# Attention in two interleaved halves, rotating product banks and a deeper weight queue in a one-core encoder step

## The chip, the cores and the metric

The kernel runs on one core of a Trainium2 chip. The core has five engines with instruction streams of their own: TensorE (in the profile PE, with its weight loads as PEld), VectorE (DVE), ScalarE (ACT), GpSimd (POOL) and SyncE (SP), which here only issues DMAs. The metric is device time in microseconds of one execution; for the kernel before, it is the median of three runs. A profile records one further execution with every instruction's start and duration.

## What is computed

One inference step of a small hybrid encoder: 512 new frames of one stream (the prompt) and 8 running streams with 16 frames each (the sample), 640 rows of width 2048 in all. A first layer (mixer A) projects 2048 to 2 x 4096, applies causal pooling over windows of 2, 4, 8 and 16 frames, a linear map per group, a gate, and projects back. Then keys, values and a forget logit per head are computed once (16 heads of 128), and a second layer (mixer B) does attention over them:

```python
def fox_attention(q, k, v, Fq, Fk, q_pos, k_pos):      # F = cumsum(log f) of the forget gates
    s = jnp.einsum('bqhd,bkhd->bhqk', qb, k) * HEAD_DIM ** -0.5
    s = s + Fq[..., None] - Fk_t[:, :, None, :]
    s = jnp.where(k_pos <= q_pos, s, -jnp.inf)
    p = jax.nn.softmax(s, axis=-1)
    o = jnp.einsum('bhqk,bkhd->bqhd', p, v)

z = rmsnorm(x) @ w_in_b                                 # queries | gate
x = x + (fox_attention(...) * silu(gate)) @ w_out_b
y = rmsnorm(x)
```

The sample rows also attend to 256 cached frames of their stream. All arrays are float32. The kernel gets float32 accuracy from three products of a faster format: each operand is split into a high and a low part (`split`, line 80: ScalarE copies the high part, VectorE subtracts), and high x high, high x low and low x high are added up.

## The kernel before

The 640 rows lie along the free dimension in two halves of 320 (`HALF`), so a product has 128 x 128 weights and 320 moving columns. TensorE's instructions run in the order in which the program writes them (`tc.manual_schedule`, line 174); the order on VectorE, ScalarE, POOL and SP is set by the framework's scheduler, ahead of time. All accumulators are slices of one tensor `banks` of eight banks (line 49).

**Input pairs and K/V pairs.** Both use a Strassen-like scheme with seven products per pair of output blocks. `pair8` (line 258) issues them for four weight slabs of 512 KB; the seven accumulators are banks 0 to 6 in the order `ORDER`, and `tbank()` gives bank 7 to transposes and other small products. `combine` (line 277) then adds and subtracts the seven banks: ScalarE copies m1, VectorE does the rest. Small pieces of other work are generators in the list `work`; `tick()` (line 88) runs the next one up to its `yield`. In `pair8` there are two ticks a slab, after products 2 and 5 (line 271), eight a pair. Thirty-one pairs belong to mixer A's input, sixteen (`kv_pair`, line 1018) to K/V.

**The forget logits** are products of the last residual stream with 16 columns of `w_kv`. `forget_sums(c)` (line 782) adds the two row blocks of stream pair c into banks 6 and 7, a strip of 32 partitions for each k mod 4, while the last output products of mixer A run. Pair 7 comes after the start of K/V: the hook of the first K/V pair calls `last_rows` (line 862), which does `forget_sums(7)`, copies the two banks to `lt`, and splits the last stream blocks. `norm_stream` (line 871) and `forget` (line 883) follow as ticks; `lt` is used in line 925.

**Attention.** Per head there is a query block and a gate block, each a projection of 2048 rows (`proj`, line 1116): four chunks of weights, 16 row blocks, six products each (`mm3`, line 1066, profile line L1069). `chunk()` (line 1111) hands over one split chunk, starts the split of one that comes later and the load of one later still. A split is a scaling of the raw weights by the norm's gain (L1090, VectorE), a copy (L1098, ScalarE) and a subtraction (L1100, VectorE); `prime()` (line 1103) leaves two split chunks in hand, in three buffers. The generator `attn(h, q_)` (line 1226) holds all of a head's attention and is run by nine ticks a projection:

- `turn_keys` transposes cached keys on VectorE (L1232); `running` (L1237) multiplies them with the sample's queries into bank 4;
- `new(t)` (line 1240) makes the scores of prompt block t in bank 4 or 5 and their softmax (L1251 to L1259), in tile `pr[t]`;
- `turn_new(t)` (line 1261) transposes `pr[t]` on TensorE into `tbank()`, here a ring of banks 6 and 7, and splits it (L1269, L1270);
- the sample's probabilities are transposed, then come its values (L1347, L1351, bank 4) and the prompt's (L1360 to L1363, bank 5);
- the result goes to `og` (L1364, L1367) and is multiplied by the gate on VectorE (L1371).

Head h's generator runs beside its own gate block and the next head's query block; the new queries may only be written when `new(3)` of head h is out (`qdone`). Loads of the next head's keys, values and sums are issued from within the generator, on SP.

**Output projection** (line 1456 on): 960 products of 512 columns; its first weights come through the same `chunk()`.

Of the kernel before, what the change touches and what calls it, by code (L numbers as in the profile page):

```python
# [17 lines left out]
P = 128  # L18
# [21 lines left out]
def tile_yoco_step(ctx, tc, i, o):  # L40
# [213 lines left out]

    def tbank():
# [484 lines left out]
    for n, (kind, g, p) in enumerate(units):  # L740
        if n == 1:
            work.append(load_cols())
        if n == 31:
# [38 lines left out]
    def forget_sums(c):  # L782
        for k in (2 * c, 2 * c + 1):
            q = k % 4
            for n in range(2):
                nc.tensor.matmul(banks[32 * q : 32 * q + 32, 6 + n, :HALF], wr[0][:, k * H : k * H + 32],
                                 stage[c][:, k % 2, n * HALF : (n + 1) * HALF], start=k < 4, stop=k >= 12)
# [21 lines left out]
    for g in range(4):  # L809
# [23 lines left out]
        dk = nd  # L833
    for j in range(4, 7):
# [17 lines left out]
    lt = pv.tile([P, NT], F32, name="lt")  # L852
    Fs = pv.tile([P, 5, H], F32, name="Fs")
# [7 lines left out]

    def last_rows():

        forget_sums(7)
        nc.scalar.activation(lt[:, :HALF], banks[:, 6, :HALF], AF.Copy)
        nc.vector.tensor_copy(lt[:, HALF:], banks[:, 7, :HALF])
# [167 lines left out]

    ones = make_ones(pv, "ones")
# [11 lines left out]
    mmring, tring = Ring([0, 2]), Ring([6, 7])  # L1047
    R = big.tile([P, NT], F32, name="R")
    dma(R, Rd)
# [9 lines left out]
    def wchunk(src, nk, nn, scale=None, pin=False):  # L1059
        raw = wp.tile([P, nk, nn], F32, tag="raw", name="raw", bufs=4)  # L1060
        dma(raw, src)
        hi, lo = (wp.tile([P, nk, nn], F32R, tag=q, name=q, bufs=3) for q in ("whi", "wlo"))
# [53 lines left out]
    def proj(ticks=9):  # L1116
# [8 lines left out]
        return pp  # L1125

# [4 lines left out]
    queue(winb, 0, nb_c)  # L1131
    for h in range(H):
        queue(winb, D + h * P, nb_c)
        if h < H - 1:
            queue(winb, (h + 1) * P, nb_c)
    for k in range(H):
        bloads.append((woutb[:, k, :512].unsqueeze(1), None))

    with ExitStack() as ctx2:
# [17 lines left out]
        def load_new_values(h):  # L1157
            vn = pb.tile([P, TT, P], F32, tag="vn", name="vn")
            dma(vn, sv[h].rearrange("(t p) d -> p t d", p=P))
            store(o["v_prompt"][0, :, h, :].rearrange("(t p) d -> p t d", p=P), vn[:, :4, :])  # L1160
# [4 lines left out]
            vals[h] = [vn, vh, vl]  # L1165
# [30 lines left out]
        def gate_block(h):  # L1196
            pp = proj(9 if h < H - 1 else 16)
# [26 lines left out]
        cached, gates, qdone = {}, [], []  # L1224

        def attn(h, q_):
            more = h < H - 1
            kc = cached[h][0]

# [31 lines left out]
            def turn_new(t):  # L1261
                kw = (t + 1) * P
                ts = slice(t * P, kw)
                a = tbank()
                for j in range(t + 1):
                    transpose(a[:, j * P : (j + 1) * P], pr[t][:, j * P : (j + 1) * P])
                n = min(t + 1, 3)
                av = a[:, : n * P].rearrange("p (j q) -> p j q", q=P)
                nc.scalar.activation(pth[:, :n, ts], av, AF.Copy)  # L1269
                nc.vector.tensor_tensor(ptl[:, :n, ts], av, pth[:, :n, ts].bitcast(F32), op=ALU.subtract)  # L1270
                if t == 3:
                    nc.scalar.activation(pt3, a[:, 3 * P :], AF.Copy)

            kct = pk.tile([P, NB * P], F32, tag="kct", name="kct")
# [3 lines left out]
            if h:  # L1278
                yield
            turn_keys(kct, 0, 1)  # L1280
            yield
            while not q_:
                yield
            qt, qh, ql, qs = q_
            kt, kh, kl = keys[h]
            fk = sums[h]
            s2 = pk2.tile([P, 2 * PAST + NS], F32, tag="s2", name="s2")
            pr = [pk2.tile([P, (t + 1) * P], F32, tag=f"p{t}", name="pr") for t in range(4)]
# [10 lines left out]
            yield  # L1299
            new(1)  # L1300
            yield
            running(ss, kct, 1)
# [13 lines left out]
            yield  # L1316
            new(2)
            pth = pk2.tile([P, 3, NP], F32R, tag="pth", name="pth")
            ptl = pk2.tile([P, 3, NP], F32R, tag="ptl", name="ptl")
            turn_new(0)  # L1320
            yield
            new(3)
            qdone.append(h)
            if more:
                split_new_keys(h + 1)
                load_sums(h + 1)
            yield
            turn_new(1)
            pt3 = pk2.tile([P, P], F32, tag="p0", name="pt3")
            yield  # L1330
            pts = pk2.tile([P, 5, P], F32, tag="pts", name="pts")
            turn_new(2)
            yield
            for js in ((0, 1, 2, 3), (4,)):
# [3 lines left out]
                nc.scalar.activation(pts[:, js[0] : js[-1] + 1].rearrange("p j n -> p (j n)"), a[:, : len(js) * P], AF.Copy)  # L1338
                yield
            turn_new(3)  # L1340
            yield
            vc = cached[h][1]
            vn, vh, vl = vals[h]
            po = banks[:, 4, :]
# [7 lines left out]
            ob = pk2.tile([P, P], F32, tag="ob", name="ob")  # L1352
            nc.vector.tensor_copy(ob, po[:, :P])
# [3 lines left out]
            op = banks[:, 5, :]  # L1357
# [5 lines left out]
            nc.tensor.matmul(op[:, 3 * P :], vn[:, 3, :], pt3, start=False, stop=True)  # L1363
            nc.scalar.activation(og[:, h, :NP], op, AF.Copy)  # L1364
            a = tbank()
            transpose(a[:, :P], ob)
            nc.scalar.activation(og[:, h, NP:], a[:, :P], AF.Copy)  # L1367
            if more:
                load_new_values(h + 1)
            sg = gates.pop()  # L1370
            nc.vector.tensor_tensor(og[:, h, :], og[:, h, :], sg, op=ALU.mult)  # L1371
# [4 lines left out]
        prime()  # L1376
        load_keys(0)
        load_new_keys(0)
        split_new_keys(0)
# [3 lines left out]
        q_ = []  # L1383
        work.append(attn(0, q_))
        for h in range(H):
            q_.extend(q_block(h))
            if h:
                work.append(attn(h, q_))
            gate_block(h)
            q_ = []  # L1390
        while work:
            tick()
# [128 lines left out]
```

## Time and profile before

| | |
|---|---|
| median of 3 runs | 2921.6 us (2912.43 to 2922.14) |
| profiled execution: time, span of its instructions | 2911.26 us, 2909.3 us |
| TensorE busy | 2780.2 us (96%) |
| VectorE busy | 2014.5 us (69%) |
| ScalarE busy | 1149.5 us (40%) |
| POOL busy | 382.2 us (13%) |
| mean granted TensorE clock | 0.985 |

Rows of groups read: line, engine, operation, output <- inputs, shapes, count | busy us, mean ns of one | idle time of the engine just before them and what ended it. Rows of time begin with start and duration in us. "Idle" of TensorE is time in which no matmul was under way; a busy TensorE can still run at a reduced clock, which the stage table shows. A line number can be that of a helper (L81 and L84 are the two halves of `split`, L105 is `transpose`).

### The profile page before, as it was taken

What the parts mean: (1) busy time and instruction counts of PE and PEld (TensorE: products, weight loads), DVE (VectorE), ACT (ScalarE), POOL (GpSimd) and SP (SyncE); (2) the same over time, 40 slices, a digit from 0 to 9 for tenths busy, and PEclk for the clock granted to TensorE, in tenths of its full rate; (3) what the DMA queues carried; (4) which work ended last, traced back from release to release, by engine and by line L of the source; (5) the groups of instructions that cost most, each with busy time, mean ns of one, the idle gap of its engine ahead of it and who ended that gap; (6) DMA issues with size and microseconds to landing.
All of it is one profiled execution on the core that took longest, in us unless ns stands there. A gap on an engine that the chain in (4) does not pass through costs nothing. (4 is left out here: it accounts for less than half of the span.)

```text
span 2909.3 us, 46312 instructions
## 1 busy us (share of the span) xinstructions
PE 2780.2 (96%) x18194; PEld 2651.2 (91%) x18194; DVE 2014.5 (69%) x3430; ACT 1149.5 (40%) x1911; POOL 382.2 (13%) x357
## 2 busy tenths in 40 slices
PE   7899999999999999999998999998999999999998
PEld 6799999999999999999998999987888888888787
DVE  7877778887786858584567888875665665656434
ACT  5433333333233435353345555542433433435222
POOL 2112131322420111112023111110000000000000
PEclk8999999999999999999999999999999999999999
DMA  3344444444345877779443554556555554545923
GB/s 124 114 130 134 132 124 129 128 131 125 112 130 164 200 166 182 171 180 182 139 145 89 117 127 117 121 123 152 138 129 128 134 131 118 133 126 110 144 85 110
DMA packets 646755, 390.69 MB, mean 134 GB/s; under 512 B 322756, under 2 KB 601716, under 8 KB 646408
## 3 DMA queue, kind: packets, MB, share of 16 engines
q1 hardware_dynamic: 626952, 333.99, 43.4%
q0 software_dynamic: 19584, 53.75, 8.6%
q8 instruction: 142, 2.33, 0.3%
q14 instruction: 77, 0.63, 0.1%
HBM read 299.66 MB, written 87.99 MB: 133 GB/s over the span
## 5 line engine op out<-in xcount | busy, mean ns | idle before, releaser
L251 PE MATMUL banks<-b,wh 128*128 128x320 f32 x2688 | 602.7, 311 | 16.7 <-ACT cve L289 10.6
L251 PE MATMUL banks<-th,wh 128*128 128x320 f32 x1792 | 566.9, 316 | 9.5 <-DVE cu L293 4.6
L251 PE MATMUL banks<-th,wl 128*128 128x320 f32 x1792 | 557.3, 311 | 2.8 <-DVE wl L84 2.8
L251 PE MATMUL banks<-tl,wh 128*128 128x320 f32 x1792 | 557.6, 311 | 0.7 <-DVE tl L84 0.7
L251 PEld LDWEIGHTS banks<-b,wh 128*128 128x128 f32 x2688 | 452.5, 189 | 18.3 <-ACT cve L289 11.6
L251 PE MATMUL banks<-b,wl 128*128 128x320 f32 x1344 | 417.2, 310 | 0.0
L84 DVE TENSOR_TENSOR wl<-raw,wh 128x768 fp32r<-128x768 f32 (+1 forms) x264 | 308.5, 1170 | 143.0 <-ACT wh L81 139.7
L81 ACT ACTIVATE wh<-sums 128x1024 fp32r<-128x1024 f32 x224 | 236.3, 1055 | 371.0 <-DVE sums L220 370.8
L81 ACT ACTIVATE wh<-raw 128x768 fp32r<-128x768 f32 (+1 forms) x264 | 230.2, 873 | 345.3 <-issue 154.8
L251 PEld LDWEIGHTS banks<-th,wh 128*128 128x128 f32 x1792 | 340.2, 190 | 19.8 <-DVE cu L293 9.1
L1069 PE MATMUL banks<-b,whi 128*128 128x320 f32 x1536 | 358.0, 317 | 0.0
L251 PEld LDWEIGHTS banks<-th,wl 128*128 128x128 f32 x1792 | 339.9, 190 | 3.3 <-DVE wl L84 3.3
L251 PEld LDWEIGHTS banks<-tl,wh 128*128 128x128 f32 x1792 | 340.2, 190 | 1.2 <-DVE tl L84 0.9
L84 DVE TENSOR_TENSOR wl<-sums,wh 128x1024 fp32r<-128x1024 f32 x224 | 282.1, 1259 | 70.6 <-ACT wh L81 70.0
L1069 PEld LDWEIGHTS banks<-b,whi 128*128 128x128 f32 x1536 | 257.8, 191 | 1.2 <-issue 0.4
L251 PEld LDWEIGHTS banks<-b,wl 128*128 128x128 f32 x1344 | 254.1, 189 | 0.0
L1069 PE MATMUL banks<-b,wlo 128*128 128x320 f32 x768 | 197.7, 312 | 0.0
L217 DVE TENSOR_TENSOR sums<-raw 128x512 f32<-128x512 f32 x236 | 174.9, 741 | 11.5 <-POOL sq L769 4.5
L1098 ACT ACTIVATE whi<-raw 128x512 fp32r<-128x512 f32 x144 | 88.9, 628 | 160.7 <-DVE raw L1090 89.8
L1100 DVE TENSOR_TENSOR wlo<-raw,whi 128x512 fp32r<-128x512 f32 x144 | 98.1, 687 | 72.6 <-ACT whi L1098 72.3
L213 ACT ACTIVATE raw<-raw,cols 128x256 f32<-128x256 f32 x256 | 111.1, 497 | 62.1 <-DMA raw<-in_w_kv 62.1
L1069 PEld LDWEIGHTS banks<-b,wlo 128*128 128x128 f32 x768 | 135.4, 190 | 0.0
(395 smaller groups left out, 4864.7 us busy)
## 6 DMA issues: line engine op xcount, KB each, us to landing
raw<-in_w_in_a SPq DMA_DIRECT2D x128, 512.0 KB, 4.0
raw<-in_w_out_a SPq DMA_DIRECT2D x64, 512.0 KB, 5.0
raw<-in_w_kv SPq DMA_DIRECT2D x64, 512.0 KB, 4.1
raw<-in_w_in_b SPq DMA_DIRECT2D x128, 256.0 KB, 3.9
raw<-in_w_grp_a SPq DMA_DIRECT2D x32, 512.0 KB, 5.6
kc<-in_cache_k SPq DMA_DIRECT2D x64, 256.0 KB, 5.3
vc<-in_cache_v SPq DMA_DIRECT2D x16, 1024.0 KB, 5.6
raw<-in_w_out_b SPq DMA_DIRECT2D x64, 256.0 KB, 3.3
```

What stands on the lines that cost most here:

```text
L81: a = nc.scalar.activation(hi, x, AF.Copy)
L84: nc.vector.tensor_tensor(lo, x, hi.bitcast(F32), op=ALU.subtract)
L213: nc.scalar.activation(raw[:, k, :], raw[:, k, :], AF.Copy, scale=loads[n][2][:, k : k + 1])
L217: nc.vector.tensor_tensor(sums[:, :, 0:2, :], raw[:, :, 1:3, :], raw[:, :, 0:1, :].to_broadcast([P, 2, 2, P]), op=ALU.subtract)
L251: nc.tensor.matmul(bank[:, :HALF], w[kk][:, a, :], x, start=first and q == 0, stop=last and q == 2)
L1069: nc.tensor.matmul(acc_[:, s, :HALF], w, stream(k, q, s), start=f, stop=l)
L1098: nc.scalar.activation(hi, raw, AF.Copy)
L1100: nc.vector.tensor_tensor(lo, raw, hi.bitcast(F32), op=ALU.subtract)
```

## The change

**Banks in rotation.** A counter `base` shifts the seven accumulators by seven banks (mod 8) after every pair, and `tbank()` is the eighth bank of the current pair. Ticks move to after products 3 and 6, and the last one of a pair is dropped, seven a pair. `base` is set to 4 before the second pair and to 2 before K/V.

**Forget sums in two parts.** Pairs 0 to 6 are copied from banks 6 and 7 to a tile `forgot` before K/V begins, stored to DRAM and loaded into `lt`. The last pair's products go to `tbank()` in the first K/V pair's hook, one half after product 3 and one after product 6, and VectorE adds them to `lt`.

**Weights.** `whi` and `wlo` get four buffers instead of three, and `prime()` leaves three split chunks. `prime()` now runs right after the weight pool exists, ahead of the loads of `R` and of `Fs`. The query block two heads ahead is queued, and the first two query blocks run before the first gate block.

**Attention in two generators.** `scoring(h)` holds the cached and new scores with their softmax, `valuing(h)` the transposes, the values and the gate product. They stand in the lists `front` and `back`; `step()` serves them in alternation, ten times a projection (sixteen in the last gate blocks). Beside gate block h-1 and query block h+1 run `scoring(h)` and `valuing(h-1)`. The set `turned[h]` tells which probability tiles have been transposed and may be rewritten. The value results use the ring of banks 6 and 7 instead of banks 4 and 5, `pt3` has a tile of its own, the split of the new values moves from their load to the middle of `valuing`, and the gate product moves from VectorE to POOL.

```diff
     def tbank():
-        return banks[:, 7, :]
+        return banks[:, (base[0] + 7) % 8, :]
...
-        pp = {m: banks[:, j, :] for j, m in enumerate(ORDER)}
+        pp = {m: banks[:, (base[0] + j) % 8, :] for j, m in enumerate(ORDER)}
...
-                if j in (2, 5):
+                if j in (3, 6) and n + j < 9:
                     tick()
+        base[0] += 7
...
+    forgot = wa.tile([P, NT], F32, tag="sums", name="forgot")
+    for n in range(2):
+        nc.scalar.activation(forgot[:, n * HALF : (n + 1) * HALF], banks[:, 6 + n, :HALF], AF.Copy)
+    lgd = dram.tile([P, NT], F32, name="lgd")
+    dma(lgd, forgot)
...
     lt = pv.tile([P, NT], F32, name="lt")
+    dma(lt, lgd)
...
+    def last_forget(n):
+        hs = slice(n * HALF, (n + 1) * HALF)
+        tb = tbank()
+        for k in (14, 15):
+            q = k % 4
+            nc.tensor.matmul(tb[32 * q : 32 * q + 32, :HALF], wr[0][:, k * H : k * H + 32], stage[7][:, k % 2, hs],
+                             start=True, stop=True)
+        nc.vector.tensor_tensor(lt[64:, hs], lt[64:, hs], tb[64:, :HALF], op=ALU.add)
...
-        forget_sums(7)
-        nc.scalar.activation(lt[:, :HALF], banks[:, 6, :HALF], AF.Copy)
-        nc.vector.tensor_copy(lt[:, HALF:], banks[:, 7, :HALF])
...
-            if (n, s, j) == (0, 0, 2):
-                last_rows()
+            if (n, s) == (0, 0) and j in (3, 6):
+                last_forget(j // 6)
+                if j == 6:
+                    last_rows()
...
-            hi, lo = (wp.tile([P, 512], F32R, tag=q, name=q, bufs=3) for q in ("whi", "wlo"))
+            hi, lo = (wp.tile([P, 512], F32R, tag=q, name=q, bufs=4) for q in ("whi", "wlo"))
...
-        split_next()
-        fetchb()
-        split_next()
-        fetchb()
+        for _ in range(3):
+            split_next()
+            fetchb()
...
+    def step():
+        turns[0] += 1
+        for q in (front, back) if turns[0] % 2 else (back, front):
+            while q:
+                try:
+                    next(q[0])
+                    return
+                except StopIteration:
+                    q.pop(0)
...
+    prime()
+    R = big.tile([P, NT], F32, name="R")
+    dma(R, Rd)
...
         def q_block(h):
             pp = proj()
-            while h and not qdone:
-                tick()
-            qdone.clear()
+            drain(front)
...
+        def valuing(h):
...
+            for t in range(4):
+                turn_new(t)
+                turned[h].add(t)
+                yield
...
-            po = banks[:, 4, :]
+            po = tbank()
...
-            op = banks[:, 5, :]
+            op = tbank()
...
-            nc.vector.tensor_tensor(og[:, h, :], og[:, h, :], sg, op=ALU.mult)
+            while not gates:
+                yield
+            nc.gpsimd.tensor_tensor(og[:, h, :], og[:, h, :], gates.pop(), op=ALU.mult)
...
-        work.append(attn(0, q_))
-        for h in range(H):
-            q_.extend(q_block(h))
-            if h:
-                work.append(attn(h, q_))
-            gate_block(h)
-            q_ = []
-        while work:
-            tick()
+        q_ = {}
+        q_[0] = q_block(0)
+        front.append(scoring(0, q_[0]))
+        q_[1] = q_block(1)
+        for h in range(1, H):
+            front.append(scoring(h, q_[h]))
+            back.append(valuing(h - 1))
+            gate_block(h - 1)
+            if h < H - 1:
+                q_[h + 1] = q_block(h + 1)
+            drain(front)
+            drain(back)
+        back.append(valuing(H - 1))
+        gate_block(H - 1)
+        drain(back)
```

More of the change, by code (lines that the diff above doesn't have):

```diff
@@ L742, in tile_yoco_step @@
             work.append(load_cols())
+            base[0] = 4
         if n == 31:
@@ L1061, in wchunk @@
         dma(raw, src)
-        hi, lo = (wp.tile([P, nk, nn], F32R, tag=q, name=q, bufs=3) for q in ("whi", "wlo"))
+        hi, lo = (wp.tile([P, nk, nn], F32R, tag=q, name=q, bufs=4) for q in ("whi", "wlo"))
         split(hi, lo, raw, pin)
@@ L1123, in proj, with drain @@
                 if kk * ticks % KT < ticks:
-                    tick()
+                    step()
         return pp
+    front, back, turns = [], [], [0]
+    def step():
[7 more added lines that the diff above has]
+                    q.pop(0)
+    def drain(q):
+        while q:
+            try:
+                next(q[0])
+            except StopIteration:
+                q.pop(0)
     def queue(src, c0, scale):
@@ L1222, in load_values, with scoring @@
             cached[h].append(vc)
-        cached, gates, qdone = {}, [], []
-        def attn(h, q_):
+        cached, gates = {}, []
+        scores = {}
+        def scoring(h, q_):
             more = h < H - 1
             kc = cached[h][0]
+            kct = pk.tile([P, NB * P], F32, tag="kct", name="kct")
             def turn_keys(kct, g, b):
@@ L1259, in new @@
                 nc.vector.tensor_scalar_mul(s, s, rw)
[L1261 to L1274, printed above, removed]
             turn_keys(kct, 0, 0)
@@ L1277, in attn @@
                 load_new_keys(h + 1)
-            if h:
-                yield
+            yield
             turn_keys(kct, 0, 1)
             yield
-            while not q_:
-                yield
             qt, qh, ql, qs = q_
+            if h == 0:
+                split_new_keys(0)
             kt, kh, kl = keys[h]
             fk = sums[h]
-            s2 = pk2.tile([P, 2 * PAST + NS], F32, tag="s2", name="s2")
-            pr = [pk2.tile([P, (t + 1) * P], F32, tag=f"p{t}", name="pr") for t in range(4)]
+            while h and 0 not in turned[h - 1]:
+                yield
+            pr = [pk2.tile([P, P], F32, tag="p0", name="pr")]
             ss = banks[:, 4, :]
@@ L1299, in attn @@
             yield
+            while h and 1 not in turned[h - 1]:
+                yield
+            pr.append(pk2.tile([P, 2 * P], F32, tag="p1", name="pr"))
             new(1)
             yield
+            while h and 5 not in turned[h - 1]:
+                yield
+            s2 = pk2.tile([P, 2 * PAST + NS], F32, tag="s2", name="s2")
             running(ss, kct, 1)
@@ L1316, in attn @@
             yield
+            pr.append(pk2.tile([P, 3 * P], F32, tag="p2", name="pr"))
             new(2)
-            pth = pk2.tile([P, 3, NP], F32R, tag="pth", name="pth")
-            ptl = pk2.tile([P, 3, NP], F32R, tag="ptl", name="ptl")
-            turn_new(0)
             yield
+            pr.append(pk2.tile([P, 4 * P], F32, tag="p3", name="pr"))
             new(3)
-            qdone.append(h)
             if more:
@@ L1326, in attn, with turn_new @@
                 load_sums(h + 1)
+            scores[h] = pr, s2
+            turned[h] = set()
             yield
-            turn_new(1)
-            pt3 = pk2.tile([P, P], F32, tag="p0", name="pt3")
-            yield
-            pts = pk2.tile([P, 5, P], F32, tag="pts", name="pts")
-            turn_new(2)
-            yield
-            for js in ((0, 1, 2, 3), (4,)):
+        turned = {}
+        def valuing(h):
+            more = h < H - 1
+            pr, s2 = scores[h]
+            pth = pk2.tile([P, 3, NP], F32R, tag="pth", name="pth")
+            ptl = pk2.tile([P, 3, NP], F32R, tag="ptl", name="ptl")
+            pt3 = pk2.tile([P, P], F32, tag="pt3", name="pt3")
+            pts = pk2.tile([P, 5, P], F32, tag="pts", name="pts")
+            def turn_new(t):
+                kw = (t + 1) * P
+                ts = slice(t * P, kw)
+                a = tbank()
+                for j in range(t + 1):
+                    transpose(a[:, j * P : (j + 1) * P], pr[t][:, j * P : (j + 1) * P])
+                n = min(t + 1, 3)
+                av = a[:, : n * P].rearrange("p (j q) -> p j q", q=P)
+                nc.scalar.activation(pth[:, :n, ts], av, AF.Copy)
+                nc.vector.tensor_tensor(ptl[:, :n, ts], av, pth[:, :n, ts].bitcast(F32), op=ALU.subtract)
+                if t == 3:
+                    nc.scalar.activation(pt3, a[:, 3 * P :], AF.Copy)
+            for t in range(4):
+                turn_new(t)
+                turned[h].add(t)
+                yield
+            for n, js in enumerate(((0, 1, 2, 3), (4,))):
                 a = tbank()
@@ L1356, in attn @@
             yield
-            op = banks[:, 5, :]
+            ob = pk2.tile([P, P], F32, tag="ob", name="ob")
+            nc.vector.tensor_copy(ob, po[:, :P])
+            op = tbank()
             for j in range(3):
@@ L1366, in attn @@
             transpose(a[:, :P], ob)
+            yield
             nc.scalar.activation(og[:, h, NP:], a[:, :P], AF.Copy)
[L1368 to L1371, printed above, removed]
+            while not gates:
+                yield
+            nc.gpsimd.tensor_tensor(og[:, h, :], og[:, h, :], gates.pop(), op=ALU.mult)
             yield
```

37 lines of the change are left out of this document (19 added, 18 removed).

## The prediction

> **What bounds the kernel now.** I read the page first, then a table of stages, then who makes TensorE wait, and last the stretches around those waits in order of time. Columns of the table: length of the stretch, busy us and instructions of each engine, granted TensorE clock, DMA share, GB/s.
>
> ```profile
> span 2909.3 us, 46312 instructions
> 83.00:886.00 803.00, 785.52 (x5267) 780.44 (x5268) 640.06 (x1019) 286.33 (x405) 201.37 (x205) 0.98 0.43 129
> 958.00:1534.00 576.00, 574.68 (x3908) 567.39 (x3906) 374.43 (x570) 230.35 (x336) 96.57 (x88) 1.00 0.69 167
> 1534.00:1957.00 423.00, 411.06 (x2733) 402.01 (x2733) 348.75 (x508) 223.28 (x389) 63.86 (x43) 0.99 0.49 117
> 1957.00:2680.00 723.00, 660.63 (x4519) 600.75 (x4520) 441.44 (x959) 273.29 (x543) 2.47 (x2) 0.98 0.53 129
> 2680.00:2910.00 230.00, 219.20 (x955) 178.45 (x953) 93.11 (x173) 59.77 (x115) 0.00 (x0) 0.98 0.54 117
> ```
>
> The stretches are mixer A's input pairs, its grouped and output products, the K/V pairs, attention (1957 to 2680) and the output projection. TensorE sets the pace in all of them; what can be won is its idle time: 723.00 - 660.63 = 62.4 us in attention, 17.5 in the input pairs, 11.9 in K/V. VectorE is busy 441.44 of 723.00 (61%) in attention, so it is late at moments and not short of time.
>
> ```profile
> PE banks L1069 <- ACT whi L1098: 36.0, 23, 5.7
> PE banks L105 <- DVE pr L1259: 22.0, 16, 2.0
> PE banks L251 <- ACT cve L289: 10.6, 4, 3.0
> PE banks L251 <- DVE cu L293: 4.6, 2, 2.4
> PE banks L1237 <- DVE kct L1232: 4.5, 2, 2.7
> PE banks L251 <- ACT ub L553: 3.8, 1, 3.8
> PE banks L251 <- DVE cu L290: 3.3, 7, 1.8
> PE banks L877 <- DVE lt L866: 2.8, 1, 2.8
> PE banks L251 <- DVE x L802: 2.3, 1, 2.3
> PE banks L105 <- DVE ptl L1270: 0.9, 1, 0.9
> ```
>
> Columns: total us, times, longest. Attention's idle time is 36.0 (projection products wait for split weights), 22.0 (the transposes of a head's probabilities wait for its softmax, once a head) and 4.5; together 62.5. The rest lies at the combines of the Strassen products and at the start of K/V.
>
> **Weights three chunks ahead.** How the 36.0 us arise, in one head:
>
> ```profile
> 2293.19 0.65 DVE L1090 TENSOR_TENSOR raw<-raw,cols 128x512 f32<-128x512 f32 x1
> 2293.94 0.63 ACT L1098 ACTIVATE whi<-raw 128x512 fp32r<-128x512 f32 x1 [2.61 <-DVE raw L1090]
> 2294.60 0.69 DVE L1100 TENSOR_TENSOR wlo<-raw,whi 128x512 fp32r<-128x512 f32 x1 [0.76 <-ACT whi L1098]
> 2294.62 0.42 PE L1069 MATMUL banks<-tl,whi 128*128 128x320 f32 x1 [1.08 <-ACT whi L1098]
> 2297.32 4.39 PE banks L1069 x30
> ```
>
> Scaling, copy and subtraction are a chain of 0.65 + 0.63 + 0.69 = 2.0 us, queued behind the new head's query and key work on VectorE. It came 1.08 us too late. One product takes 4.39 / 30 = 0.146 us, and a chunk has 24 of them, so a third chunk in hand gives 24 x 0.146 = 3.5 us more slack, without the attention work between. That exceeds each wait but the first (5.7), which stands at the hand-over from K/V. There the first weight loads now precede the load of R and of Fs on SP, which I take to win half. Term: -31; bounds -36 (all gone) to 0 (the split is put off just as long). The added split at the start is one 2.0 us chain, inside the hand-over.
>
> **Scores of one head beside values of its neighbour.** The transposes now use probabilities finished a phase earlier, so the wait for L1259 has about a head's time, 723 / 16 = 45 us, for cover. By the order of the steps, scoring needs 9 turns and valuing 11, and a phase (gate block, then query block) offers 10 + 10 = 20: they fit with nothing to spare. The gates `turned` hold at once, because valuing's transposes of index t are always one or more turns ahead of scoring's rewrite of that tile. Term: -21 of 22.0; bounds -22 to 0. Of the 4.5 us for kct, 2.7 stand at the tail and 1.8 at the start; -2, bounds -4.5 to +2.
>
> The stalls also cost clock:
>
> ```profile
> 2314.97 0.55 PE L105 MATMUL banks<-ident,pr 128*128 128x128 f32 x3 [2.04 <-DVE pr L1259]
> 2315.28:2317.97 2.69, 2.69 (x12) 2.69 (x12) 0.59 0.25 64
> ```
>
> After 2.04 us of idle time, 12 products took 2.69 us where 12 x 0.146 = 1.75 is usual, at a granted clock of 0.59. The stage's mean clock of 0.98 says 0.02 x 723 = about 14 us in all, of which I take 10 back, for two slow stretches may stay at the start and tail. Term: -10; bounds -14 to 0. [...]
>
> New costs. A head's attention work went to TensorE in 13 pieces between projection products (scores and transposes of t = 2 and 0 shared a turn, so did values and the last transpose); now it is 15. What a piece costs beyond its work:
>
> ```profile
> 2357.49 0.31 PE L1069 MATMUL banks<-b,wlo 128*128 128x320 f32 x1
> 2357.64 0.38 PE L105 MATMUL banks<-ident,pr 128*128 128x128 f32 x2
> 2357.78 0.82 PE L1069 MATMUL banks<-b,whi 128*128 128x320 f32 x4
> ```
>
> Two transposes push the projection back by 0.14 us and its next four take 0.82 us where 3 x 0.146 + 0.31 = 0.75 is usual: 0.2 us for a whole piece, work included. So 2 x 16 x 0.15 = +5; bounds 0 to +10. The end: in the last phase there are 16 turns for 20 pieces, so some four run without products beside them; a score's wait for its bank is at most the waits of 2.0 and 2.7 seen above, so +3, bounds 0 to +8.
>
> The product with the gate moves to POOL:
>
> ```profile
> L1371 DVE TENSOR_TENSOR og<-og,sgb 128x640 f32<-128x640 f32 x15 | 12.4, 826 | 60.2 <-ACT og L1367 60.2
> 1540.71 2.22 POOL L769 TENSOR_TENSOR sq<-sq 128x640 f32<-128x640 f32 x1 [2.01 <-ACT sq L768]
> 687.76 3.77 POOL L568 TENSOR_TENSOR sw<-sw 128x768 f32<-128x768 f32 x2
> 688.27 1.57 DVE L219 TENSOR_TENSOR sums<-sums,raw 128x256 f32<-128x256 f32 x1
> 695.55 0.42 DVE L219 TENSOR_TENSOR sums<-sums,raw 128x256 f32<-128x256 f32 x1
> ```
>
> VectorE is rid of 0.826 us a head; POOL takes up to 2.22 us for that shape. Beside POOL's additions VectorE's L219 took 1.57 us instead of 0.42, so 16 heads may give VectorE back up to 16 x 1.15 = 18 us. VectorE has 723.00 - 441.44 = 282 us idle, and the weights now have 3.5 us more cover, so I price it at 0; bounds -2 to +18 if that cover is gone. [...]
>
> **Rotated product banks (input pairs, K/V).** A pair's first product now goes into the bank that the last pair left free, and every other into the bank of the product before it. So each combine step gets the time of one product, 6 x 0.146 = 0.88 us, more.
>
> ```profile
> 697.43 0.42 ACT L289 ACTIVATE cve<-banks 128x320 f32<-128x320 f32 x1
> 698.70 0.48 DVE L290 TENSOR_TENSOR cu<-cve,banks 128x320 f32<-128x320 f32 x1
> ```
>
> In the four waits of 2.6 to 3.0 us that make 10.6, the first copy is itself late (VectorE beside POOL, above), and the second step follows 1.3 us on. So 0.88 of each goes, and with a shorter stall perhaps the slow clock behind it (another 1 us): 4 x 1.9 = 8. Of L293, L290 and L553 (4.6 + 3.3 + 3.8) I take 3, since the early pairs then wait for weights instead. The turns fall from 8 to 7 a pair; the work queued needs fewer, and the last turn, whose bank the next pair would want, is the one left out. Term: -11; bounds -22 (all four rows) to +5.
>
> **The forget sums at the start of K/V.** Instead of reading banks 6 and 7 at once, the sums go to `forgot` (in the buffer of the squares, tag sums), to DRAM and back; two last products are then added on VectorE. This puts a chain in TensorE's way:
>
> ```profile
> 1542.96 0.69 DVE L217 TENSOR_TENSOR sums<-raw 128x512 f32<-128x512 f32 x1 [1.43 <-POOL sq L769]
> 1544.66 1.41 PE L877 MATMUL banks<-sq,ones 128*128 128x320 f32 x2 [2.79 <-DVE lt L866]
> dscr<-dd POOLq DMA_DIRECT2D x32, 320.0 KB, 2.5
> R<-Rd SPq DMA_DIRECT2D x1, 320.0 KB, 2.9
> ```
>
> That buffer came free at 1542.96, after the last square was added on POOL. From there: two copies like L289 (0.8), out 2.5, back 2.9: lt is there at about 1549. Until then the first addition stands on VectorE, the second product on TensorE (same bank) behind it, and all later pairs behind that; SP's weight loads stand behind the load of lt. Before, TensorE was past 1544.66. About 5 us new, plus some wait for banks 6 and 7 earlier, against 2.8 (L866) and 2.3 (L802) removed: +4. Bounds: -5 (POOL adds the square earlier) to +12.
>
> **The sum.** -31 - 21 - 2 - 10 + 5 + 3 + 0 - 11 + 4 = -63. The profiled execution took 2911.26 us (span 2909.3 and 2.0 around it), so 2848. The median of the runs is 2921.6, 0.36% above that execution; the same ratio gives **2858 us**.
>
> **Rivals.**
> 1. *The splits stay late.* VectorE's order is fixed ahead, and it may place the third split as late as the second was. For:
>
> ```profile
> 2284.63 0.29 DVE L1353 COPY ob<-banks 128x128 f32<-128x128 f32 x1 [5.09 <-PE banks L1351]
> 2288.99 0.83 DVE L1371 TENSOR_TENSOR og<-og,sgb 128x640 f32<-128x640 f32 x1 [4.07 <-ACT og L1367]
> ```
>
> VectorE stood idle for 5.09 + 4.07 us shortly before the late split above, behind instructions that came first in its order. Against: the extra chunk gives just such an order more time. Then 31 stay: 2848 + 31 = 2879, as a median 2889.
> 2. *The change doesn't do what it says.* 20 turns for 20 pieces: one missed turn a phase leaves the last scores to the drain, where softmax and banks stand open as L1259 did (2.0 us), and the weight waits stay as well: -63 + 31 + 21 + 10 = -1 or so. Median about 2920. Against: I find no turn that is spent on waiting.
> 3. *Slower: the two banks of the ring (6, 7).* Values and their outputs move from banks 4 and 5 into the ring, so a head uses it 9 times, and each use must be copied out by ScalarE and VectorE before the second next one. If VectorE's order puts these copies behind the other head's softmax, TensorE waits at each of 9 x 15 = 135 uses. Above (63 + 15) / 135 = 0.58 us each the kernel is measurably slower; at 0.7 us it is 2848 + 95 = 2943, median 2953. For: softmax and copies now mix. Against: the row L105 <- L1270 shows 0.9 us for this wait in the whole run, in the same two banks.
>
> **Chances.** My forecast 0.74, splits late 0.12, no gain 0.07, slower 0.07. Within the likeliest case, weights at -20, banks at -4 and forget sums at +9 give 2858 + 11 + 7 + 5 = 2881; banks at -22, forget sums at -5 and pieces at 0 give 2858 - 11 - 9 - 5 = 2833, and some of the 5 us left at the hand-over may go too. Rival 1 (2889) is taken in; the two others are left out. Range **2825 to 2900**. Under 0.5% (14.6 us) a measurement of this kernel can't be told from no change. Faster 0.86, same 0.07, slower 0.07.
>
> **What would show it.** Right: no wait for L1098 over 1 us between 2000 and 2600 and none of the transposes for the softmax; mean clock 0.99 or 1.00 in attention; its stretch near 665 us; the waits for the first copy of a combine 0.9 us shorter each; a new TensorE wait of some us for the forget sums near 1540. Wrong: many waits for the ring's copies, whi waits of the old size, or an attention period still near 45 us a head.

## The result, and the profile after

The changed kernel takes **2845.8 us** (median of 4 runs, 2844.21 to 2847.46) against 2917.0 for the kernel before on the same chips: a ratio of **0.9757, 95% interval 0.9731 to 0.9784**. The forecast was 2858 in a range of 2825 to 2900. The profiled execution took 2844.21 us with a span of 2842.5, that is 66.8 less than the 2909.3 of before; the sum of the prediction was 63.

Line numbers have moved: the projection product is L1086 (was L1069), its split L1107, L1115, L1117 (was L1090, L1098, L1100), the cached keys L1277 and L1282, the copy out of the ring L1385 (was L1270), the output projection L1479 (was L1413). First the same table of stages, cut at the first product of each; columns as before.

```profile
78.80:885.20 806.40, 784.59 (x5277) 779.69 (x5276) 645.51 (x1026) 292.08 (x412) 200.63 (x205) 0.99 0.44 130
885.20:1531.20 646.00, 645.11 (x4376) 637.59 (x4376) 425.09 (x650) 258.51 (x366) 96.19 (x88) 1.00 0.67 165
1531.20:1957.40 426.20, 406.51 (x2736) 402.95 (x2734) 357.47 (x513) 226.25 (x394) 65.61 (x44) 0.98 0.50 119
1957.40:2607.00 649.60, 643.47 (x4512) 595.86 (x4513) 441.84 (x942) 270.69 (x541) 23.62 (x15) 1.00 0.57 142
2607.00:2842.50 235.50, 221.91 (x962) 180.85 (x960) 92.08 (x171) 61.59 (x116) 1.59 (x1) 0.98 0.52 114
```

In attention TensorE is busy 643.47 of 649.60 us at a clock of 1.00; before it was 660.63 of 723.00 at 0.98. VectorE is busy there for as long as before (441.84 us against 441.44): what differs is above all the place of its work in time. Who makes TensorE wait, over the whole run:

```profile
PE banks L1086 <- ACT whi L1115: 7.8, 2, 5.7
PE banks L251 <- ACT forgot L840: 6.6, 1, 6.6
PE banks L251 <- ACT cve L292: 6.2, 3, 2.3
...
PE banks L251 <- DVE wl L84: 4.3, 4, 2.1
PE banks L669 <- DVE cve L294: 3.9, 1, 3.9
PE banks L251 <- ACT pq L601: 3.8, 1, 3.8
...
PE banks L877 <- DVE lt L879: 3.0, 1, 3.0
PE banks L1479 <- DVE wlo L84: 2.9, 2, 2.3
PE banks L251 <- ACT wh L81: 2.5, 2, 1.7
PE banks L1479 <- ACT whi L81: 2.1, 1, 2.1
PE banks L893 <- DVE lt L879: 1.7, 1, 1.7
PE banks L1282 <- DVE kct L1277: 1.6, 2, 0.9
```

The 36.0 us for split weights are 7.8, of which 5.7 is the hand-over from K/V, as long as before. The 22.0 us for the softmax are gone. New are the waits for the forget sums (L840, L879), for a copy out of the transposes' bank (L601), at the first grouped product (L669) and at the start of the second column block of the output (L1479).

The stages of the traces, from the first product of each to the first of the next (hand-over: last product of K/V to first of attention; attention ends with its last product or transpose):

| us | input pairs | grouped | K/V | hand-over | attention | output |
|---|---|---|---|---|---|---|
| before (starts at 82.9) | 804.5 | 647.6 | 420.4 | 6.0 | 718.5 | 229.5 |
| after (starts at 78.8) | 806.4 | 646.1 | 420.1 | 6.0 | 649.5 | 235.6 |

So attention gives 69.0, everything ahead of it 3.9, the hand-over nothing, and the output projection takes 6.1 back. (The profile's table above is cut at 1531.20, the last grouped product; the first K/V product starts 0.1 us later, and in the kernel before it started at 1534.94.) Two profiles of the changed kernel differ by 2.8 us in the pairs (the second has 803.6).

### The profile page after: what moved, and what is told of

Read it like the earlier page. It is cut to its first block, busy times and chain, and to the rows that moved or that the text cites. A ratio compares the mean times of both kernels' runs of the same rounds, so it can differ in the third digit from the quotient of the medians.

```text
span 2842.5 us, 46301 instructions
## 1 busy us (share of the span) xinstructions
PE 2760.4 (97%) x18194; PEld 2649.7 (93%) x18194; DVE 2019.7 (71%) x3415; ACT 1151.2 (41%) x1912; POOL 404.8 (14%) x373
## 4 chain that ended last, share of the span: by engine, by line
PE 43%; DVE 4%; DMA 2%; ACT 1%; issue 1%; POOL 1%; SPq 0%; DVEq 0%; ACTq 0%; POOLq 0%
PE banks L1086 15%; PE banks L251 9%; PE banks L1479 7%; PE banks L669 5%; PE banks L1407 2%; DVE wl L84 2%; PE banks L1282 1%; DMA raw<-in_w_kv 1%; PE banks L105 1%; ACT wh L81 0%; DMA raw<-in_w_grp_a 0%; PE banks L1422 0%; PE banks L1421 0%; PE banks L1420 0%; PE banks L1292 0%
## 5 line engine op out<-in xcount | busy, mean ns | idle before, releaser
L251 PE MATMUL banks<-th,wh 128*128 128x320 f32 x1792 | 559.8, 312 | 9.1 <-ACT cve L292 6.2
L251 PE MATMUL banks<-tl,wh 128*128 128x320 f32 x1792 | 557.3, 311 | 0.7 <-DVE tl L84 0.7
L84 DVE TENSOR_TENSOR wl<-raw,wh 128x768 fp32r<-128x768 f32 (+1 forms) x264 | 307.4, 1165 | 145.0 <-ACT wh L81 144.5
L81 ACT ACTIVATE wh<-raw 128x768 fp32r<-128x768 f32 (+1 forms) x264 | 230.6, 875 | 379.9 <-issue 138.2
L81 ACT ACTIVATE wh<-sums 128x1024 fp32r<-128x1024 f32 x224 | 236.2, 1054 | 340.5 <-DVE sums L220 340.1
L1086 PE MATMUL banks<-b,whi 128*128 128x320 f32 x1536 | 355.4, 315 | 0.0
L84 DVE TENSOR_TENSOR wl<-sums,wh 128x1024 fp32r<-128x1024 f32 x224 | 281.5, 1257 | 59.9 <-ACT wh L81 59.5
L1086 PEld LDWEIGHTS banks<-b,whi 128*128 128x128 f32 x1536 | 254.8, 189 | 1.6 <-issue 0.2
L1086 PE MATMUL banks<-b,wlo 128*128 128x320 f32 x768 | 196.1, 310 | 0.0
L217 DVE TENSOR_TENSOR sums<-raw 128x512 f32<-128x512 f32 x236 | 172.4, 730 | 14.6 <-DMA raw<-in_w_out_a 3.5
L1115 ACT ACTIVATE whi<-raw 128x512 fp32r<-128x512 f32 x144 | 90.0, 628 | 151.9 <-PE banks L1086 56.3
L669 PE MATMUL banks<-th,wh 128*128 128x320 f32 x576 | 132.3, 311 | 4.4 <-DVE cve L294 3.9
L1086 PEld LDWEIGHTS banks<-b,wlo 128*128 128x128 f32 x768 | 133.9, 188 | 0.0
L669 PE MATMUL banks<-tl,wh 128*128 128x320 f32 x576 | 131.8, 310 | 0.0
```

The lines of the kernel that those rows point to most:

```text
L81: a = nc.scalar.activation(hi, x, AF.Copy)
L84: nc.vector.tensor_tensor(lo, x, hi.bitcast(F32), op=ALU.subtract)
L217: nc.vector.tensor_tensor(sums[:, :, 0:2, :], raw[:, :, 1:3, :], raw[:, :, 0:1, :].to_broadcast([P, 2, 2, P]), op=ALU.subtract)
L251: nc.tensor.matmul(bank[:, :HALF], w[kk][:, a, :], x, start=first and q == 0, stop=last and q == 2)
L669: nc.tensor.matmul(bk[s], w, x[:, s * HALF : (s + 1) * HALF], start=k + q == 0, stop=k == 7 and q == 2)
L1086: nc.tensor.matmul(acc_[:, s, :HALF], w, stream(k, q, s), start=f, stop=l)
```

## The experiments

Theory A is the prediction's: the weight waits and the softmax waits are two things, and each half of the change removes one. Theory B, its rival, is that both come from one cause, and the division of attention alone removes both.

**1. Three chunks ahead, in the old attention.**

```diff
-            hi, lo = (wp.tile([P, 512], F32R, tag=q, name=q, bufs=3) for q in ("whi", "wlo"))
+            hi, lo = (wp.tile([P, 512], F32R, tag=q, name=q, bufs=4) for q in ("whi", "wlo"))
...
-        split_next()
-        fetchb()
-        split_next()
-        fetchb()
+        for _ in range(3):
+            split_next()
+            fetchb()
```

The same number of buffers in `wchunk`, which splits the later weights of the output projection, changes with it, here and in the next run.

> The kernel before with four weight buffers and three chunks split ahead; nothing else is changed. Theory A (two separate waits): the waits of the projection products for split weights (36.0 us) fall to the 5.7 us of the hand-over and little else, the softmax wait (22.0 us) stays; about 31 us less than before plus two or three slow-clock stretches, so a ratio near 0.987. Theory B (one cause: the old generator makes VectorE late in bursts, and only the division into halves cures it): the chunk split in advance is put off as long, the weight waits stay above 25 us, ratio 0.997 to 1.00.

Measured: 2903.1 us, ratio 0.9966 (0.9954 to 0.9977). TensorE's waits in the steady part of attention (2002 to 2640), before and then with the third chunk:

```profile
PE banks L1069 <- ACT whi L1098: 27.3, 21, 2.8
PE banks L105 <- DVE pr L1259: 20.0, 14, 2.0
PE banks L105 <- DVE ptl L1270: 0.9, 1, 0.9
```

```profile
PE banks L105 <- DVE pr L1258: 19.9, 15, 1.6
PE banks L105 <- DVE ptl L1269: 15.5, 15, 1.0
PE banks L1246 <- DVE s L1304: 6.2, 13, 0.5
PE banks L1069 <- ACT whi L1098: 1.5, 1, 1.5
```

The weight wait did what theory A said, 27.3 to 1.5. The time did not follow: 15.5 us came up at the copy out of the ring and 6.2 at the sample's scores, 0 to 1 us each before. The waits changed their name; 48.2 us of them became 43.1. Attention went from 718.5 to 704.1 and the output projection from 229.5 to 233.4. Theory A's number falls, and so does B's picture of a split that is put off as long.

**2. The two halves, with two chunks ahead.**

```diff
-            hi, lo = (wp.tile([P, 512], F32R, tag=q, name=q, bufs=4) for q in ("whi", "wlo"))
+            hi, lo = (wp.tile([P, 512], F32R, tag=q, name=q, bufs=3) for q in ("whi", "wlo"))
...
-        for _ in range(3):
+        for _ in range(2):
             split_next()
```

> The changed kernel with three weight buffers and two chunks split ahead again. Theory A: the weight waits come back, some 20 to 31 us, ratio to before 0.983 to 0.987. Theory B: the halves alone remove both waits, the time stays within 4 us of the changed kernel, ratio 0.975 to 0.977.

Measured: 2845.4 us, ratio 0.9770 (0.9753 to 0.9786), no different from the changed kernel. Between 2002 and 2560 TensorE has no wait at all. Over the whole run the weight row is

```profile
PE banks L1086 <- ACT whi L1115: 12.8, 2, 7.1
```

that is, the hand-over and one wait of 7.1 us at the start of attention. Attention takes 659.5 us instead of 649.5, the output projection 231.6 instead of 235.6. So the new attention removes both waits without the third chunk, as theory B said, and the third chunk has only the start to help with: there it saves 8 to 10 us of attention (a second profile of the changed kernel has 651.8), 5 of them in this row.

**3 and 4. Old banks and forget sums ahead of the new attention, and the reverse.** The programs of before and after are each cut at the line `wp = pool(ctx, "wp")` and put together crosswise; only the first bank pair of the projections is matched to the banks that are free (`Ring([0, 2])` or `Ring([2, 0])`).

> The changed kernel's attention and output projection behind the old fixed banks, old ticks and old forget sums. If the banks win 11 us and the forget sums lose 4, as forecast, this run is about 7 us slower than the changed kernel (ratio to before 0.978). If the two cancel, as the stages of the trace suggest (the start of the grouped products came 2.2 us earlier, that of attention 3.9), it is 2 to 5 us slower. If the forget sums outweigh the banks, it is faster than the changed kernel.

> The complement: rotated banks, new ticks and the new forget sums ahead of the old attention. The same reading: 0 to 7 us faster than before (ratio 0.9975 to 1.000). Its time won and that of the run with the old banks should add up to the whole 71 us if the two parts don't touch each other.

Measured: 2850.4 us, 0.9785 (0.9770 to 0.9800), for the old banks with the new attention; 2903.2 us, 0.9971 (0.9961 to 0.9982), for the new banks with the old attention. Won are 2.15% and 0.29%; together 2.44%, and the whole change won 2.43%. Within these intervals the parts don't touch each other, and banks with forget sums are worth about 8 us (0.29% of 2912; 5 to 11 by the interval), near the 7 us of the prediction's -11 + 4.

**5. The changed kernel again**, for the three runs beside it.

> The changed kernel itself, on the chip of the three runs beside it, so that differences of a few us can be read; 2843 to 2849 us.

Measured: 2842.1 us, ratio 0.9762 (0.9746 to 0.9778).

**6. Another place for the forget sums.**

```diff
-    forgot = wa.tile([P, NT], F32, tag="sums", name="forgot")
+    forgot = bslot(7, [P, NT])
```

> The changed kernel with the tile of the forget sums in the buffer of the last stream block (tag b7), which is free by then, instead of the buffer of the squares (tag sums). If the stall at the start of K/V comes from that buffer, as forecast, the wait for the copy of the forget sums (6.6 us) falls below 1 us, the trip to DRAM and back starts some 8 us earlier, and the run is 6 to 10 us faster than the changed kernel. If it comes from POOL's or ScalarE's own order, or if the time goes into the next wait (the DRAM trip), it is 0 to 3 us faster.

In the changed kernel's trace the chain is (ScalarE's copy, SP's load back, VectorE's first addition, and ahead of them POOL's last square):

```profile
1539.58 2.21 POOL L773 TENSOR_TENSOR sq<-sq 128x640 f32<-128x640 f32 x1 [2.01 <-ACT sq L772]
1541.83 0.77 ACT L840 ACTIVATE forgot<-banks 128x320 f32<-128x320 f32 x2 [1.43 <-POOL sq L773]
1545.05 0.34 SPq L862 DMA_DIRECT2D lt<-lgd  x1
1549.91 0.49 DVE L879 TENSOR_TENSOR lt<-lt,banks 64x320 f32<-64x320 f32 x1
```

That is the chain of the prediction, to 1549.91 where "about 1549" was expected; the wait ahead of it, for the banks, was 6.6 us and so larger than the "some" it allowed for. Measured with the other place: 2840.8 us, 0.9759 (0.9744 to 0.9773), that is 1.3 us below the changed kernel on the same chip, inside the noise. Its waits and its chain:

```profile
PE banks L877 <- DVE lt L879: 6.5, 1, 6.5
```

```profile
1534.11 0.41 SPq L862 DMA_DIRECT2D lt<-lgd  x1
1540.42 0.69 DVE L217 TENSOR_TENSOR sums<-raw 128x512 f32<-128x512 f32 x1 [1.42 <-POOL sq L773]
1543.22 0.49 DVE L879 TENSOR_TENSOR lt<-lt,banks 64x320 f32<-64x320 f32 x1
```

The copy's wait is gone and the trip to DRAM begins 11 us earlier, but in VectorE's fixed order the addition stands behind the weight sums L217, and these still wait for POOL's last square. The stall has moved by one link.

**7 and 8. The product with the gate: back on VectorE in the new kernel, and alone on POOL in the old one.**

```diff
-            nc.gpsimd.tensor_tensor(og[:, h, :], og[:, h, :], gates.pop(), op=ALU.mult)
+            nc.vector.tensor_tensor(og[:, h, :], og[:, h, :], gates.pop(), op=ALU.mult)
```

> The changed kernel with the product with the gate back on VectorE. If VectorE's time is hidden, as forecast, within 2 us of the changed kernel. If VectorE's place in the order counts (it stands before this product until ScalarE has copied the head's result, 4.07 us a head before the change), weight waits or waits at the ring come back in each head, 10 us or more slower.

> The kernel before with only the product with the gate moved to POOL. The run with four weight buffers alone showed that the weight waits of the old order can go without the time going with them. If they arise because VectorE stands before the gate product (4.07 us a head) and only then begins the next head's queries and weights, they fall by 15 us or more here and the run is 10 to 20 us faster than before. If they arise from the bunching of one head's softmax, values and the next head's queries as such, the run stays within 4 us of before.

Measured: 2841.4 us, 0.9759 (0.9745 to 0.9774), for the first; 2912.0 us, 1.0000 (0.9990 to 1.0009), for the second, with the old waits in full:

```profile
PE banks L1069 <- ACT whi L1098: 35.4, 23, 5.7
PE banks L105 <- DVE pr L1259: 21.4, 15, 2.0
```

The engine of this product doesn't matter in either order. VectorE's 4.07 us in front of it were slack and not the cause of the late splits.

**9. Values first, then scores.** What is left as a cause is how a head's work on VectorE is spread. VectorE in the steady part, in one of the emptiest and in the fullest 15 us of it: the kernel before, then the changed one.

```profile
2002.00:2640.00 638.00, 386.09 (x847) 0.99 0.52 128
2318.50:2333.50 15.00, 1.62 (x4) 0.98 0.40 114
2438.50:2453.50 15.00, 14.02 (x34) 1.00 0.90 190
```

```profile
2002.00:2560.00 558.00, 375.14 (x807) 1.00 0.57 143
2307.00:2322.00 15.00, 6.62 (x16) 1.00 0.55 159
2453.50:2468.50 15.00, 12.41 (x27) 1.00 0.64 139
```

Before, VectorE was idle but for 1.62 us in one stretch and full to 14.02 of 15 us in another; now it runs between 6.62 and 12.41. The experiment keeps the division, with two chunks ahead and three buffers as in run 2, and gives up the alternation:

```diff
-        for q in (front, back) if turns[0] % 2 else (back, front):
+        for q in (back, front):
```

> The changed kernel with two chunks split ahead and three buffers, and with the turns given to valuing until it is done and only then to scoring, instead of in alternation. The work is the same, in the same phases, but all softmax work now falls into the query block. If the weight waits come from bunched work on VectorE (in the trace of before its busy share in stretches of 15 us runs from 0.12 to 0.95, in that of the changed kernel from 0.48 to 0.87), waits of TensorE for split weights or for the softmax come back in each head: 10 us or more slower than the run with two chunks (2845), ratio to before above 0.980. If it is enough that scores and values of a head lie in different phases, the ratio stays at 0.977.

Measured: 2911.5 us, 1.0001 (0.9992 to 1.0010). **All of the gain is gone**, attention is at 726.2 us, and VectorE's fullest stretch is at 14.62 again:

```profile
2092.50:2107.50 15.00, 1.54 (x3) 0.97 0.22 64
2471.00:2486.00 15.00, 14.62 (x37) 1.00 0.99 232
```

```profile
PE banks L105 <- DVE ptl L1385: 31.4, 15, 3.8
PE banks L1086 <- DVE wlo L1117: 6.2, 14, 0.8
PE banks L1086 <- ACT whi L1115: 5.5, 7, 0.8
```

(The last three are TensorE's waits between 2002 and 2640.) Weight waits came back, 11.7 us of them, but the larger part is the ring, with one wait a head: as four transposes now stand in turns that follow one another, a bank must be copied out within one turn and not within three. Why the copy is late shows at one such place (the first row has the busy time of TensorE, its weight loads, VectorE, ScalarE and POOL in that stretch):

```profile
2305.00:2315.00 10.00, 8.00 (x57) 7.71 (x56) 9.49 (x23) 5.30 (x14) 0.00 (x0) 1.00 0.55 135
2306.68 0.25 ACT L1384 ACTIVATE pth<-banks 128x128 fp32r<-128x128 f32 x1
2311.51 0.61 DVE L1385 TENSOR_TENSOR ptl<-banks,pth 128x128 fp32r<-128x128 f32 x2
2311.84 0.55 PE L105 MATMUL banks<-ident,pr 128*128 128x128 f32 x3 [2.00 <-DVE ptl L1385]
```

ScalarE has copied the first transpose's bank by 2306.93. VectorE's subtraction, which sets the bank free, runs at 2311.51, behind 4.6 us of softmax, key, query and weight work with one gap of 0.17 us. Short turns alone don't make this wait: in the kernel before, most uses of the ring follow turn upon turn too, and its row for the ring is 0.9 us. So it is the mechanism of the prediction's third rival, copies that stand behind softmax on VectorE, at one of a head's nine uses.

**10. The same with three chunks ahead** (the changed kernel with the one line above).

> The changed kernel with its three chunks ahead, but values first and scores after them, as in the run before it with two chunks, where TensorE waited 34.7 us for the copies out of the ring and 18.3 + 6.2 us for split weights (12.8 of the 18.3 also with alternating turns). If the third chunk is cover against bunched work, the 6.2 and some 5 to 10 of the 18.3 go and the run is 8 to 15 us faster than that one (ratio to before 0.995 to 0.997). If the waits only change their name, as they did in the old order, the ratio stays at 0.998 or more, with longer waits at the ring or for the softmax.

Measured: 2913.2 us, 1.0004 (0.9995 to 1.0014).

```profile
PE banks L105 <- DVE ptl L1385: 42.1, 15, 4.6
PE banks L1086 <- ACT whi L1115: 20.9, 15, 5.7
```

The third chunk wins nothing here; the waits for copies out of the ring are 42.1 us over the run (34.7 with two chunks). In both arrangements with bunched work, this one and the old attention of run 1, it shifted waits, for a gain of nothing and of 9 us.

**11 and 12. The remaining stalls mended**, with three and with two chunks. The edits: `forgot` in the other place and the sums of stream block 6 on VectorE; the first grouped product into the free bank; the pool state's transposes a turn earlier; the last K/V pair scaled by R on VectorE; two splits of the next output columns ahead of the row sums.

```diff
-            sums_t(x4of(j), None, nc.gpsimd)
+            sums_t(x4of(j))
...
-    bank8 = [0]
+    bank8 = [5]
...
-            for _ in range(4):
+            for _ in range(3):
                 yield
...
+        if n == 15:
+            for b in range(2):
+                nc.vector.tensor_tensor(t[:, b, :], t[:, b, :], R, op=ALU.mult)
+        else:
             nc.gpsimd.tensor_tensor(t, t, R.unsqueeze(1).to_broadcast([P, 2, NT]), op=ALU.mult)
...
+                if n < 2:
+                    ahead = [wchunk(woutb[:, k, (n + 1) * 512 : (n + 2) * 512].unsqueeze(1), 1, 512) for k in range(2)]
```

> The changed kernel with the stalls mended that its trace still shows: the forget sums in buffer b7 and the sums of stream block 6 on VectorE (so that the last squares are not behind POOL's 5.6 us); the first bank of the grouped products is the free one (5), not one that the last combine still reads; the transposes of the pool state one turn earlier; the last K/V pair scaled by R on VectorE in two halves instead of POOL (2.9 us ahead of the first weights of attention); two weight splits of the next output column block ahead of the row sums. Expected by the waits in the trace: 4 to 8 at K/V, 3 at the grouped products, 2 to 4 at the pool state, 2 at the hand-over, 3 to 5 in the output: 2826 to 2834, if the time does not go into the next wait, as it did when only the forget sums were moved.

> The same with two chunks split ahead and three buffers (and one split ahead in the output). If the third chunk is worth nothing once the halves are apart, as the run with two chunks says, within 3 us of the run with all mends.

Measured: **2829.0 us, 0.9715 (0.9702 to 0.9729)**, and 2833.8 us, 0.9727 (0.9713 to 0.9740). Both are faster than the changed kernel's 2842 to 2846. In the trace with three chunks the pairs take 798.8 us, K/V 413.3, the hand-over 4.2 and the output still 236.0. Its longest waits at these places:

```profile
PE banks L877 <- DVE lt L879: 7.2, 1, 7.2
PE banks L1090 <- ACT whi L1119: 6.1, 2, 3.9
...
PE banks L1483 <- DVE wlo L84: 2.3, 1, 2.3
PE banks L1483 <- ACT whi L81: 2.1, 1, 2.1
```

The hand-over's wait fell from 5.7 to 3.9. The output's splits stayed as late as they were, and the addition of the forget sums still waits 7.2 us. The two-chunk version is 4.8 us behind, with intervals that overlap, so the third chunk is worth between nothing and some 5 us.

## Why the prediction was right, and where its steps were not

**The whole: right**, 63 us forecast on the span and 66.8 found, faster as forecast, inside the range. The likeliest case came about: in the steady part neither weights nor softmax are waited for. That the total came so near is in part luck: attention gave 69.0 us where the terms for it add up to 56 (31 + 21 + 2 + 10 - 5 - 3), all ahead of it gave 3.9 in place of 7, and the output projection took back 6.1 that no term foresaw.

**Weights three chunks ahead (-31): the step that failed.** The row fell by 28.2 us, near the forecast, but not through the third chunk: the two generators in alternation do it without one (runs 2 and 9), and the third chunk alone wins 9 us (run 1). The prediction read 36.0 and 22.0 us as two waits with a cause each, since they stand in two rows. They were one shortage: a head's work on VectorE in a bunch, whose lateness showed wherever TensorE next needed something. At the 2.04 us wait that the prediction shows, ScalarE has the exponentials at 2313.15, but VectorE, without a gap since 2310.67, reaches their scaling (L1259) only at 2314.51, behind work for another score block, the next keys and the gate; in run 9 the copies of the ring stand in the same kind of queue. "3.5 us more slack" was true and moved the wait to the next place.

**Scores beside values (-21 and -2): right in mechanism and too small.** The softmax row went from 22.0 us to nothing, the keys from 4.5 to 1.6. To it belong the weight waits too. The count of turns, 20 for 20, agrees with the yields in the code.

**Slow clock (-10): right.** Attention's mean clock rose from 0.98 to 1.00. The trace before has seven stretches of 3.4 us at a clock of 0.50 there, which cost 11.6 us; after the change one is left, at the start, for 1.6 us.

**Pieces (+5) and end (+3): too large.** Of attention's 69.0 us, 51.9 are idle time of TensorE (from 58.0 to 6.1, the hand-over left out) and 17.1 are busy time (from 660.58 to 643.47). The clock accounts for 10 of the 17; where the other 7 come from is open, but a cost of the two further pieces can't be seen. After 2560 three waits remain at the tail, for keys (0.7 us), the ring (0.8) and results (1.2).

**The hand-over (half of 5.7): wrong.** The weight loads are indeed earlier, and it doesn't matter:

```profile
1948.71 2.06 SPq L1101 DMA_DIRECT2D raw<-in_w_in_b  x4
1955.31 0.84 DVE L1024 STREAM_TRANSPOSE kn<-x 128x640 f32<-128x640 f32 x1 [3.00 <-POOL x L1050]
1956.08 1.25 DVE L1107 TENSOR_TENSOR raw<-raw,cols 128x512 f32<-128x512 f32 x2
```

The scaling stands on VectorE behind a transpose that waits 3.00 us for POOL's product with R. The prediction saw the queue on SP and missed the one on VectorE. With that product on VectorE (run 11) the wait falls to 3.9.

**Rotated banks (-11) and forget sums (+4): right in sum, by luck in the parts.** Together some 8 us won by runs 3 and 4, where 7 were expected. But the waits for the first copy of a combine, which were to give 8, gave 4.4 (10.6 to 6.2), and the rows of L293, L290 and L553, of which 3 were taken, went almost whole (11.7 to 0.4). L553 was the wait ahead of the first of these pairs, so the stage starts 4.1 us earlier. The pairs themselves take as long as before: waits for split weights grew (L84 and L81, 3.7 to 6.8), and two new waits came at the seams, for a transposed state's copy (3.8, L601) and at the first grouped product, whose bank the last combine still read (3.9). The prediction said that the dropped turn kept the first of these out; it is the turn before, now a pair's last, that causes it, for with these transposes one turn earlier (run 11) the wait is gone. The forget sums' chain came out as worked out, and its waits are 11.3 us (6.6 + 3.0 + 1.7) in place of 5.1 (2.8 + 2.3).

**Gate on POOL (0): right**, by runs 7 and 8.

**Not foreseen: the output projection, +6.1.** Its second column block waits 5.0 us for weights split late (2.9 + 2.1, L1479). It goes with the third chunk and the fourth buffer: in each of the four pairs of runs that differ in these, the output takes longer with them (233.4 against 229.5 in the old attention, 235.6 against 231.6 in the new, 236.0 against 233.2 with values first, 236.0 against 230.1 with the stalls mended). Why they make the splits late stays open; two splits placed ahead did not cure it.

**Open as well:** how much of the alternation's gain is VectorE's spread work, and how much the longer time a bank of the ring has. Run 9 takes both away at once; its trace shows a full VectorE ahead of the late copy, but no run changes the one without the other.

## What to carry to other kernels

Waits that stand in several rows can be one shortage of one engine at one time. Before adding the rows up as separate gains, look at that engine's busy share in short stretches; a mean of 61% held stretches of 11% and 93% here. Deeper buffers then rename the wait (here 48.2 us of waits became 43.1, run 1), while alternating two independent strands in the order of issue removes it (here to none between 2002 and 2560, run 2), and the alternation is worth testing by itself.

In a program whose engines have fixed orders, an early load, a free bank or a faster engine helps only up to the next instruction in that order that waits for something else (here 1.3 us, inside the noise, for the free buffer of run 6, and nothing for the earlier weight loads at the hand-over): read the queue of each engine on the way, not only the one that was changed.

## What the runs showed of the hardware

In the kernel before, TensorE's granted clock was 0.59 in the 2.7 us behind a wait of 2.04 us (2315.28 to 2317.97). Between 2002 and 2640 of that trace TensorE waited seven times for 2.03 us or longer. Behind four of these waits (2.81, 2.04, 2.03 and 2.03 us, up to 2028.72, 2314.97, 2404.15 and 2493.30) the clock was 0.50 for 3.4 us; behind the three others (2.03 us each, up to 2139.75, 2227.36 and 2582.42), and behind every wait of 1.50 us or less, it stayed at 1.00. In the changed kernel, with TensorE busy 99% of attention (643.47 of 649.60), the granted clock was 1.00, so denser work cost no clock on this one core.

Products of 128 x 128 weights and 320 columns of float32 (L877, four in the kernel before) lasted 0.43 us at the shortest; those of the split parts lasted 0.31 us in the median (L1069).

Moving a two-input product of 128 x 640 between VectorE and POOL, sixteen times, changed nothing that can be measured (2841.4 us on VectorE against 2842.1 on POOL in run 7; a ratio of 1.0000 in run 8), in kernels in which VectorE was busy 61% of attention (441.44 of 723.00, the product on VectorE) and 68% (441.84 of 649.60, on POOL).
